# Index queries for the last 384 of 512 real tokens, in a one-core hybrid retention and sparse-attention block

## The chip, the cores and the metric

The kernel runs on one core of a Trainium2 chip. The metric is the device time of one execution in microseconds; the median of three runs is compared. Engines are named as in the profile: PE is the matrix engine (PEld its weight loads), DVE the vector engine, ACT the scalar engine, POOL the general engine, SP the queue that issues most loads.

## The reference

One layer on 512 real tokens behind 16 meta tokens (528 positions, width 1024), all in float32: a feed-forward block, a mixer, a second feed-forward block, a final norm. The mixer projects the normed input once with `w_in` and splits it into retention (rq, rk, rv, rg), attention (aq, ak, av), the index (iq, ik, iw) and two gates. What matters here is the index of the sparse attention:

```python
rel = jax.nn.relu(jnp.einsum('bqhd,bsd->bqhs', qib, ki))
score = jnp.einsum('bqh,bqhs->bqs', wib, rel).astype(jnp.float32) * idx_scale
admissible = (key_pos[None, :] >= N_META) & (key_pos[None, :] <= tq[:, None])
score = jnp.where(admissible[None], score, -jnp.inf)
_, sel = lax.top_k(score, k_top)          # k_top = min(256, 512 // 4) = 128
```

Each query keeps the 128 real keys with the highest scores among those at or before it, and always the meta keys. A query among the first 128 real tokens has at most 128 admissible keys, so it keeps them all, whatever their scores are. Index queries are 8 heads of 64, rotated by position (rope); the index key is one head of 64.

## The kernel before

Activations lie transposed, features on the partitions and tokens along the columns: `xs(k)` gives two tiles of 128 x 528 for each of 8 blocks of features, a high part `xh` and a remainder `xl`, so that a float32 product is made of three matmuls in a rounded format. Weights come as raw blocks of two column groups (`load_w`, issued on SP, two buffers `raw`) and are split by `split_w` into `whi` (ACT, line 117) and `wlo` (DVE, line 118), three buffers each. `mm3` (line 152) then runs, for one group of 128 output features, 8 x 3 matmuls into one PSUM tile. `REAL = slice(NM, T)` picks the columns of the 512 real tokens.

The kernel runs feed-forward 1, then the index projections, then retention over 4 heads, attention over 8 heads, the output projections and feed-forward 2. The order of PE's instructions is the order of the program text (a manual schedule for PE); those of the other engines are ordered by the framework's scheduler, with its own priorities, and then run in that order.

The index stage (lines 565 to 600) is this. PE projects four groups of index queries (`psiq`), each two heads, and keeps all four in the four banks of the pool `sm`. Between them stand the pieces of the mixer's norm: after the first group ten small matmuls `psn` (line 204) sum the squares `ssum` that POOL has added up; DVE and POOL make the reciprocal roots (lines 211, 213), DVE spreads them on a diagonal (218, 222) and it is split; after the third group four matmuls `psn` (line 228) turn it into `R`, which ACT copies out (line 229). POOL multiplies the rope tables `cos` and `sin` with `R` (527, 528). `rope_swap` then rotates each group: four copies of swapped halves on ACT (547, 548), a product with cos on DVE (549) that ends the use of the bank, a product with sin on POOL (550), a sum on DVE (551); `split` makes `iqh` and `iql` of it. Then follow the index keys and the head weights, projected together (`psik`), and rotated likewise into `ikh` and `ikl`.

`index_steps` computes the scores later, a step at a time between the projections of retention (`psrq`, `psrk`, `psrg`, `psrv`), only for the query blocks j = 3, 2, 1 of 128 tokens, and `select_steps` picks the top 128 by 16 rounds of eight maxima for the same three blocks. Block 0 needs neither: its bias is the causal mask. So the first 128 columns of each index query are computed and never read.

Of the kernel before, what the change touches and what calls it, by code (L numbers as in the profile page):

```python
# [12 lines left out]
F32R = mybir.dt.float32r  # L13
# [5 lines left out]
P = 128  # L19
D = 1024  # L20
KD = D // P
S = 512
NM = 16
T = S + NM
# [57 lines left out]
def kernel(ctx: ExitStack, tc: tile.TileContext, x, meta, g1, wg1, wu1, wd1, gm,  # L82
# [53 lines left out]
    def split_w(v, eng=nc.vector):  # L136
        nk, n = v.shape[1], v.shape[2]
        hi = wpool.tile([P, 1024 + WPAD], F32R, tag="whi", name="whi", bufs=3)[:, w_at[0] :]
        lo = wpool.tile([P, 1024 + WPAD], F32R, tag="wlo", name="wlo", bufs=3)[:, w_at[0] :]
        hv = hi[:, : nk * n].rearrange("p (k c) -> p k c", k=nk)  # L140
        lv = lo[:, : nk * n].rearrange("p (k c) -> p k c", k=nk)
        split(v, hv, lv, eng)
        return hv, lv

    def mm3(outs, w, xs, nk, first=True, last=True):

        wh, wl = w
        for k in range(nk):
            xh, xl = xs(k)
            for i, (a, b) in enumerate(((wh, xh), (wh, xl), (wl, xh))):  # L150
                for o, sl in outs:
                    nc.tensor.matmul(o, a[:, k, :], b[:, sl], start=first and k == 0 and i == 0,  # L152
                                     stop=last and k == nk - 1 and i == 2)
# [21 lines left out]
    def new_x(k, at=0):  # L175

        h = xpool.tile([P, TX], F32R, tag=f"xh{k}", name=f"xh{k}")[:, at : at + T]
        l = xpool.tile([P, TX], F32R, tag=f"xl{k}", name=f"xl{k}")[:, at : at + T]
        xs_now[k] = (h, l)
        return h, l  # L180

    def xs(k):
        return xs_now[k]

    REAL = slice(NM, T)

    def halves(t, cut=TH):

        a, b = t[:, 512 - cut : 512], t[:, 512 : 512 + T - cut]
        return [(a, slice(0, cut)), (b, slice(cut, T))], t[:, 512 - cut : 512 - cut + T]  # L190
# [45 lines left out]
    def add_square(h, ssum, first, tpool, n=T, bufs=2, eng=nc.gpsimd):  # L236
        if first:
            nc.scalar.activation(ssum[:, :n], h, AF.Square)
        else:
            sq = tpool.tile([P, wide(n)], F32, tag="sq", name="sq", bufs=bufs)  # L240
            nc.scalar.activation(sq[:, :n], h, AF.Square)
            eng.tensor_tensor(ssum[:, :n], ssum[:, :n], sq[:, :n], ALU.add)
# [13 lines left out]
    with pool("f1") as fp, pool("gps", 2, PSUM) as gps, ExitStack() as later:  # L256
# [5 lines left out]
        def mm_tile(name):  # L262

            i = mm_count[0]
            mm_count[0] += 1
            return mm_pools[i % len(mm_pools)].tile([P, 1024], F32, tag="mm", name=name)
# [106 lines left out]
        with tc.manual_schedule(engines={mybir.EngineType.PE, mybir.EngineType.Activation, mybir.EngineType.DVE}):  # L373
            pss = [mm_tile("psg"), mm_tile("psg")]
# [87 lines left out]
        for f0, nf in ((0, 12), (12, 10)):  # L462
            hid = []
            for f in range(f0, f0 + nf, 2):
                cg = slice(f * P, (f + 2) * P)
                if f:
                    raw = load_w(wg1[:, cg], KD, 2 * P)
                    pss = []
                    for i in range(2):
                        w = split_w(raw[:, :, i * P : (i + 1) * P])  # L470
                        ps = mm_tile("psg")
# [15 lines left out]
                for i in range(2):  # L487
                    if f:
                        w = split_w(raw[:, :, i * P : (i + 1) * P])
                        ps = mm_tile("psu")  # L490
                        mm3(halves(ps)[0], w, xs, KD)
                    else:
                        ps = psus[i]
# [7 lines left out]
            for c in range(0, KD, 2):  # L501
                pss = [mm_tile("psd") for _ in range(2)]
                for kk in range(2):
                    r0 = (f0 + kk * nk) * P
                    raw = load_w(wd1[r0 : r0 + nk * P, c * P : (c + 2) * P], nk, 2 * P)
                    for i in range(2):
                        w = split_w(raw[:, :, i * P : (i + 1) * P])
                        mm3(halves(pss[i])[0], w, lambda k: hid[kk * nk + k], nk, kk == 0, kk == 1)
                for i in range(2):
                    k = c + i  # L510
                    nc.vector.scalar_tensor_tensor(hT[k], halves(pss[i])[1], 0.5, hT[k], ALU.mult, ALU.add)
                    if f0:
                        h, l = new_x(k, XO)
                        split_gain(hT[k], gains[:, 1, k : k + 1], h, l)
                        add_square(hT[k], ssum2, k == 0, fp, bufs=4)
                        nc.scalar.dma_start(hd[k], hT[k][:, REAL])
    R = R2
    Rr = R[:, REAL]
    w_at[0] = 0
# [15 lines left out]
    def sm_tile(name):  # L535
        return smp.tile([P, S], F32, tag="sm", name=name)
# [4 lines left out]
    def rope_swap(ps, cos, sin, half, n):  # L541

        a, b = tmp(), tmp()
        av, bv = a[:, :n], b[:, :n]
        for r in range(0, P, 2 * half):
            lo, hi = slice(r, r + half), slice(r + half, r + 2 * half)
            nc.scalar.activation(bv[hi], ps[lo], AF.Copy)
            nc.scalar.activation(bv[lo], ps[hi], AF.Copy)
        nc.vector.tensor_tensor(av, ps, cos, ALU.mult)
        nc.gpsimd.tensor_tensor(b[:, :n], b[:, :n], sin, ALU.mult)  # L550
        nc.vector.tensor_tensor(a[:, :n], a[:, :n], b[:, :n], ALU.add)
        return a[:, :n]
# [9 lines left out]
    ix = ixs.enter_context(pool("ix", 1, side="right"))  # L562


    with pool("ixt") as ixt:
        tp.update(pool=ixt, bufs=8)
        norm = rstd_steps(ssum2, T, D, R2, ixt, lambda: mm_tile("psn"))
        pss = []
        cols = Cols(w_in, OFF_IQ, 4)
        for i in range(4):  # L570
            w = cols.next()
            ps = sm_tile("psiq")
            mm3([(ps, REAL)], w, xs, KD)
            pss.append(ps)
            if i < 3:
                next(norm)
        cos, sin = rope_tables(0, ixt)
        iq = []
        for i in range(4):
            y = rope_swap(pss[i], cos[:, REAL], sin[:, REAL], 32, S)  # L580
            h = ix.tile([P, S], F32R, tag=f"iqh{i}", name="iqh")
            l = ix.tile([P, S], F32R, tag=f"iql{i}", name="iql")
            split(y, h, l)
            iq.append((h, l))
        w = Cols(w_in, OFF_IK, 1).next()
        ps = sm_tile("psik")
        mm3([(ps, REAL)], w, xs, KD)
        a, y = tmp(), tmp()
        nc.scalar.activation(y[32:64, :S], ps[0:32], AF.Copy)
        nc.scalar.activation(y[0:32, :S], ps[32:64], AF.Copy)  # L590
        nc.vector.tensor_tensor(a[0:64, :S], ps[0:64], cos[0:64, REAL], ALU.mult)
        iw = ix.tile([IH, S], F32, tag="iw", name="iw")
        nc.vector.tensor_tensor(iw, ps[64:72], R[64:72, REAL], ALU.mult)
        nc.gpsimd.tensor_tensor(y[0:64, :S], y[0:64, :S], sin[0:64, REAL], ALU.mult)
        nc.vector.tensor_tensor(y[0:64, :S], a[0:64, :S], y[0:64, :S], ALU.add)
        ikh = ix.tile([P, S], F32R, tag="ikh", name="ikh")
        ikl = ix.tile([P, S], F32R, tag="ikl", name="ikl")
        for r in (0, 64):
            nc.scalar.activation(ikh[r : r + 64], y[0:64, :S], AF.Copy)
            nc.vector.tensor_tensor(ikl[r : r + 64], y[0:64, :S], ikh[0:64].bitcast(F32), ALU.subtract)  # L600
    wt = bp.tile([P, 4, IH], F32, tag="wt", name="wt")

    def index_steps():
        psw = sm_tile("psw")
        for j in range(1, 4):
            nc.tensor.transpose(psw[:, j * IH : (j + 1) * IH], iw[:, j * P : (j + 1) * P], ident[:IH, :IH])
        nc.scalar.activation(wt[:, 1:4, :], psw[:, IH : 4 * IH].rearrange("p (j h) -> p j h", h=IH),
                             AF.Copy, scale=float(np.float32(ID**-0.5) * np.float32(IH**-0.5)))
        for j in (3, 2, 1):
            n = P * (j + 1)  # L610
            for h0 in range(0, IH, 2):
                qh, ql = iq[h0 // 2]
                qs = slice(j * P, (j + 1) * P)
                pair = [sm_tile("pssc") for _ in range(2)]
                for i, (a, b) in enumerate(((qh, ikh), (qh, ikl), (ql, ikh))):
                    for ps, r in zip(pair, (0, 64)):
                        nc.tensor.matmul(ps[:, :n], a[r : r + 64, qs], b[r : r + 64, :n], start=i == 0, stop=i == 2)
                for h, ps in enumerate(pair, h0):
                    rel = tmp()
                    nc.scalar.activation(rel[:, :n], ps[:, :n], AF.Relu)  # L620
                    nc.vector.scalar_tensor_tensor(
                        score[j], rel[:, :n], wt[:, j, h : h + 1],
                        caus[:, S - n :] if h == 0 else score[j], ALU.mult, ALU.add)
                    yield
# [52 lines left out]
    with pool("rt") as rt:  # L677
        tp.update(pool=rt, bufs=7)
        cos, sin = rope_tables(2, rt)
# [201 lines left out]
    with pool("ao") as ao:  # L881
        ao_parts = []
        with pool("at") as at:
            tp.update(pool=at, bufs=8)
            cos, sin = rope_tables(1, at)
# [109 lines left out]
        with pool("ou") as ou:  # L995
# [5 lines left out]
            for c in range(KD):  # L1001
                w = cols.next()
                ps = sm_tile("psga")
# [6 lines left out]
            for c in range(KD):  # L1010
                w = cols.next()
                ps = sm_tile("psat")
# [11 lines left out]
    with pool("om") as ou:  # L1024
# [10 lines left out]
        for c in range(KD):  # L1035
            hc = ou.tile([P, S], F32, tag="hc", name="hc", bufs=4)
            nc.scalar.dma_start(hc, hd[c])
            w = cols.next()
            ps = sm_tile("psmo")
# [4 lines left out]
            h, l = new_x(c)  # L1044
# [10 lines left out]
        for i in range(2):  # L1055
            w = split_w(raw0[:, :, i * P : (i + 1) * P])
# [13 lines left out]
    with pool("f2") as fp, pool("f2ps", 8, PSUM) as f2ps:  # L1070
# [30 lines left out]
        for f0, nf in ((0, 12), (12, 10)):  # L1101
            hid = []
            for f in range(f0, f0 + nf, 2):
                cg = slice(f * P, (f + 2) * P)
                if f:
                    raw = load_w(wg2[:, cg], KD, 2 * P)
                    ps = [bank("psg") for _ in range(2)]
                else:
                    ps = ps0
                st = []  # L1110
                for i in range(2):
                    if f:
                        w = split_w(raw[:, :, i * P : (i + 1) * P])
# [7 lines left out]
                ps = [bank("psu") for _ in range(2)]  # L1121
                for i in range(2):
                    w = split_w(raw[:, :, i * P : (i + 1) * P])
# [7 lines left out]
            for c in range(2):  # L1131
                cs = slice(c * 512, (c + 1) * 512)
                pss = [bank("psd") for _ in range(4)]
# [48 lines left out]
```

## Time and profile before

| | |
|---|---|
| median of 3 runs | 1594.84 us (1594.56 to 1595.37) |
| the profiled execution | 1595.39 us |
| its span | 1593.5 us, granted PE clock 0.999 |
| PE, DVE, ACT, POOL busy | 99%, 52%, 36%, 15% of the span |
| index stage, psiq to psik's start | 397.4 to 421.1 us |
| moved by DMA | 148.66 MB, mean 93 GB/s |

A row of the timeline gives start, duration in us, engine, line, operation, `out<-in` by tile names, then the array's rows and columns in use, the moving operand's partitions x columns, and the count; in brackets the engine's idle time before and what ended it. Matmul durations are modelled and overlap each other; a matmul's cost is read from the distance between starts. A row of a group ends with total busy us, mean ns of one, and idle time before it.

### The profile page before, as it was taken

The numbers are of one execution on the slowest core, as the hardware profiler recorded it, in microseconds if no ns is written. First come the engines' busy times: TensorE is split into PE (matmuls) and PEld (weight loads), VectorE is DVE, ScalarE is ACT, GpSimd is POOL, SyncE is SP. The second block draws the span as 40 slices with busy tenths as digits, with TensorE's granted clock in tenths as the row PEclk, the third lists the DMA queues.
The fourth block names the chain that finished last, engine by engine and source line by source line (L and its number), as shares of the span: only waits on it lengthen the run. The fifth ranks groups of instructions, "written<-read, shape, count | busy, mean of one in ns | idle before, by whom it ended". The sixth has DMA issues, their size and how long they took to land.

```text
span 1593.5 us, 23010 instructions
## 1 busy us (share of the span) xinstructions
PE 1582.4 (99%) x9731; PEld 1421.5 (89%) x9731; DVE 820.9 (52%) x1263; ACT 570.6 (36%) x912; POOL 232.7 (15%) x187
## 2 busy tenths in 40 slices
PE   9999999999999999999999999999999999999998
PEld 8999999999888898899898999988888888888886
DVE  5443234334575776866845666753454434324434
ACT  6322222233544333233333555553234323223223
POOL 1211001111320200301304210011002111001100
PEclk9999999999999999999999999999999999999999
DMA  5222232224332132231312322313243322232222
GB/s 185 90 84 83 93 113 80 97 80 143 108 112 67 42 116 78 80 116 40 119 54 72 112 69 66 94 58 103 80 138 101 118 96 89 89 113 90 93 91 81
DMA packets 148582, 148.66 MB, mean 93 GB/s; under 512 B 3288, under 2 KB 137456, under 8 KB 148480
## 3 DMA queue, kind: packets, MB, share of 16 engines
q1 hardware_dynamic: 143872, 138.16, 26.9%
q10 hardware_dynamic: 4544, 9.03, 1.7%
q8 instruction: 76, 1.25, 0.3%
q14 instruction: 26, 0.21, 0.0%
q0 software_dynamic: 64, 0.01, 0.0%
HBM read 143.00 MB, written 4.19 MB: 92 GB/s over the span
## 4 chain that ended last, share of the span: by engine, by line
PE 91%; DVE 4%; ACT 2%; issue 1%; POOL 1%; DMA 1%; ACTq 0%; POOLq 0%; DVEq 0%
PE psu L152 15%; PE psg L152 15%; PE psd L152 8%; PE psd L1143 7%; PE psrv L152 6%; PE psrg L152 6%; PE psrk L152 3%; PE psgate L152 3%; PE psmo L152 3%; PE psat L152 3%; PE psga L152 3%; PE psak L152 3%; PE psav L152 3%; PE psrq L152 2%; PE psro L152 2%; PE psaq L152 2%
## 5 line engine op out<-in xcount | busy, mean ns | idle before, releaser
L117 ACT ACTIVATE whi<-raw 128x1024 fp32r<-128x1024 f32 (+3 forms) x284 | 277.7, 979 | 841.8 <-PE psu L152 165.6
L118 DVE TENSOR_TENSOR wlo<-raw,whi 128x1024 fp32r<-128x1024 f32 (+3 forms) x284 | 338.6, 1192 | 179.0 <-ACT whi L117 175.3
L152 PE MATMUL psu<-xl,whi 128*128 128x264 f32 (+1 forms) x528 | 141.0, 319 | 0.0
L152 PE MATMUL psu<-xh,whi 128*128 128x264 f32 (+1 forms) x528 | 140.6, 318 | 0.0
L152 PE MATMUL psu<-xh,wlo 128*128 128x264 f32 (+1 forms) x528 | 140.6, 318 | 0.0
L152 PE MATMUL psg<-xl,whi 128*128 128x264 f32 (+1 forms) x496 | 133.3, 321 | 0.0
L152 PE MATMUL psg<-xh,wlo 128*128 128x264 f32 (+1 forms) x496 | 132.8, 321 | 0.0
L152 PE MATMUL psg<-xh,whi 128*128 128x264 f32 (+1 forms) x496 | 132.8, 320 | 0.0
L152 PEld LDWEIGHTS psu<-xh,wlo 128*128 128x128 f32 x528 | 88.1, 188 | 6.9
L152 PEld LDWEIGHTS psu<-xh,whi 128*128 128x128 f32 x528 | 87.8, 188 | 6.8
L152 PEld LDWEIGHTS psu<-xl,whi 128*128 128x128 f32 x528 | 87.4, 188 | 6.9
L152 PEld LDWEIGHTS psg<-xh,wlo 128*128 128x128 f32 x496 | 82.6, 188 | 6.9
L152 PEld LDWEIGHTS psg<-xh,whi 128*128 128x128 f32 x496 | 82.3, 188 | 6.7
L152 PEld LDWEIGHTS psg<-xl,whi 128*128 128x128 f32 x496 | 82.0, 188 | 6.8
L483 POOL TENSOR_TENSOR t<-t,R 128x528 f32<-128x528 f32 x22 | 37.5, 1707 | 262.3 <-ACT t L482 262.3
L1118 POOL TENSOR_TENSOR t<-t,R 128x512 f32<-128x512 f32 x22 | 38.4, 1748 | 251.6 <-ACT t L1117 251.6
L152 PE MATMUL psd<-hl,whi 128*128 128x264 f32 x352 | 71.3, 284 | 0.0
L152 PE MATMUL psd<-hh,wlo 128*128 128x264 f32 x352 | 70.8, 283 | 0.0
L152 PE MATMUL psd<-hh,whi 128*128 128x264 f32 x352 | 70.6, 282 | 0.0
L1143 PE MATMUL psd<-whi,hh 128*128 128x512 f32 x176 | 68.5, 389 | 0.0
L1143 PE MATMUL psd<-wlo,hh 128*128 128x512 f32 x176 | 68.5, 389 | 0.0
L1143 PE MATMUL psd<-whi,hl 128*128 128x512 f32 x176 | 68.5, 389 | 0.0
(316 smaller groups left out, 3555.8 us busy)
## 6 DMA issues: line engine op xcount, KB each, us to landing
raw<-in_w_in_dram SPq DMA_DIRECT2D x34, 1024.0 KB, 4.9
raw<-in_ffn_w_up_dram SPq DMA_DIRECT2D x22, 1024.0 KB, 5.0
raw<-in_ffn_w_gate_dram SPq DMA_DIRECT2D x21, 1024.0 KB, 5.0
raw<-in_w_in_dram SPq DMA_DIRECT2D x25, 512.0 KB, 3.5
raw<-in_ffn_w_down_dram SPq DMA_DIRECT2D x10, 1024.0 KB, 4.8
raw<-in_w_ret_out_dram SPq DMA_DIRECT2D x16, 512.0 KB, 3.4
raw<-in_ffn_w_down_dram SPq DMA_DIRECT2D x8, 768.0 KB, 4.3
raw<-in_ffn_w_down_dram SPq DMA_DIRECT2D x8, 640.0 KB, 3.9
```

Of the source, the lines that this page charges most:

```text
L117: nc.scalar.activation(hi, src, AF.Copy)
L118: eng.tensor_tensor(lo, src, hi.bitcast(F32), ALU.subtract)
L152: nc.tensor.matmul(o, a[:, k, :], b[:, sl], start=first and k == 0 and i == 0, stop=last and k == nk - 1 and i == 2)
L483: nc.gpsimd.tensor_tensor(t, t, R, ALU.mult)
L1118: nc.gpsimd.tensor_tensor(t, t, R, ALU.mult)
L1143: nc.tensor.matmul(pss[b], a[:, bs], m[:, k % 2, :], start=k0 + k == 0 and i == 0, stop=k0 + k == nf - 1 and i == 2)
```

## The change

The index queries are projected, rotated and split for the last 384 real tokens alone. The moving operand of the 96 `psiq` matmuls starts 128 columns later and is 384 columns wide instead of 512; so are the copies, products, sums and casts of the four groups, and the tiles `iqh` and `iql`. The scores read the same queries under a slice shifted by 128. Index keys, head weights, scores and selection are as before.

```diff
     REAL = slice(NM, T)
+
+    LATE = slice(NM + P, T)
+    NL = S - P
...
-            ps = sm_tile("psiq")
-            mm3([(ps, REAL)], w, xs, KD)
+            ps = sm_tile("psiq")[:, :NL]
+            mm3([(ps, LATE)], w, xs, KD)
...
-            y = rope_swap(pss[i], cos[:, REAL], sin[:, REAL], 32, S)
-            h = ix.tile([P, S], F32R, tag=f"iqh{i}", name="iqh")
-            l = ix.tile([P, S], F32R, tag=f"iql{i}", name="iql")
+            y = rope_swap(pss[i], cos[:, LATE], sin[:, LATE], 32, NL)
+            h = ix.tile([P, NL], F32R, tag=f"iqh{i}", name="iqh")
+            l = ix.tile([P, NL], F32R, tag=f"iql{i}", name="iql")
...
-                qs = slice(j * P, (j + 1) * P)
+                qs = slice((j - 1) * P, j * P)
```

## The prediction

> **What bounds the kernel now.** I read the page first: busy time by engine, then the chain that ended last.
>
> ```profile
> PE 1582.4 (99%) x9731; PEld 1421.5 (89%) x9731; DVE 820.9 (52%) x1263; ACT 570.6 (36%) x912; POOL 232.7 (15%) x187
> ...
> PE 91%; DVE 4%; ACT 2%; issue 1%; POOL 1%; DMA 1%; ACTq 0%; POOLq 0%; DVEq 0%
> ```
>
> TensorE (PE) is busy for 99% of the span, and 91% of the chain is its matmuls; there is one weight load for each matmul. What PE no longer has to stream comes off the end, unless something that fed it in time now comes too late. So the stage of the change has to be read closely. The timeline of PE from 397 us on:
>
> ```profile
> 397.42 0.40 PE L152 MATMUL psiq<-xh,whi 128*128 128x512 f32 x1
> ...
> 402.65 0.40 PE L152 MATMUL psiq<-xh,wlo 128*128 128x512 f32 x1
> 402.88 1.17 PE L204 MATMUL psn<-ones,ssum 128*128 128x1 f32 x10
> ...
> 414.92 0.75 PE L228 MATMUL psn<-tmp,ones_r 128*128 128x512 f32 x4
> ...
> 421.09 0.39 PE L152 MATMUL psik<-xh,whi 128*128 128x512 f32 x1
> ...
> 432.20 0.39 PE L152 MATMUL psrq<-xl,whi 128*128 128x512 f32 x1
> 432.74 0.50 PE L152 MATMUL psrq<-xh,wlo 128*128 128x512 f32 x1
> ```
>
> First column: start; second: modelled duration, which overlaps the next one, so what a matmul costs is the distance between starts. The first index-query group takes 402.88 - 397.42 = 5.46 us for 24 matmuls, 0.2275 each. PE goes through four groups, the two small psn pieces of the norm, psik and psrq without a gap, up to one: the matmul due at 432.20 + 0.23 = 432.43 starts at 432.74, 0.31 late. The list of waits names what it waited for:
>
> ```profile
> PEld psrq L152 <- DVE wlo L118: 0.6, 1, 0.6
> ```
>
> **The term that is removed.** 96 matmuls (4 tiles x 8 k x 3 parts) go from 512 to 384 columns. No matmul of that shape with 128 rows stands in this trace; the same timeline has 400 and 272 columns in one stretch:
>
> ```profile
> 464.49 0.34 PE L751 MATMUL psst<-rqh,rkh 128*128 128x400 f32 x1
> ...
> 465.57 0.29 PE L751 MATMUL psst<-rqh,rkh 128*128 128x272 f32 x1
> ...
> 466.31 0.28 PE L751 MATMUL psst<-rqh,rkh 128*128 128x256 f32 x1
> ```
>
> Six of 400 columns take 465.57 - 464.49 = 1.08 us, 0.180 each; six of 272 take 0.74, 0.123 each. That is 0.44 ns a column between 272 and 400, and (0.2275 - 0.180) / 112 = 0.42 between 400 and 512: one straight line. At 384 it gives 0.180 - 16 x 0.43 ns = 0.173. The saving is 96 x (0.2275 - 0.173) = 5.2 us. The ends: not less than if 384 cost what 400 costs, 96 x 0.0475 = 4.6; not more than 96 x 128 x 0.44 ns = 5.4. I take 5.2, since 384 is nearest to the row of 400 and three rows agree on the slope. The distance of 0.123 also says that a weight load, though it lasts longer, does not set the pace:
>
> ```profile
> L152 PEld LDWEIGHTS psu<-xh,wlo 128*128 128x128 f32 x528 | 88.1, 188 | 6.9
> ```
>
> [...]
>
> **What PE now reaches earlier, in order.** Each time below is the old one minus what PE has saved by then.
>
> *The column sums.* The rows of the weight load that PE does ahead of psn, and of the POOL add that makes its operand:
>
> ```profile
> 402.65 1.32 PEld L204 LDWEIGHTS psn<-ones,ssum 128*128 128x128 f32 x10
> ```
> ```profile
> 399.79 1.82 POOL L242 TENSOR_TENSOR ssum<-ssum,sq 128x528 f32<-128x528 f32 x1 [1.82 <-ACT sq L241]
> ```
>
> The first group now ends 24 x 0.0545 = 1.3 us earlier; the weight load is due at 401.34, but ssum is complete at 401.61. A wait that was covered by streaming is uncovered: 0.27 plus a signal, so 0.3 us, with every later matmul queued behind it. Bounds: 0 (if the load need not come so early: the matmul itself is due at 401.57) to 0.6. From here all of PE is 1.0 earlier, after psiq 1 and 2 (0.055 x 48 = 2.6 more) 3.6, and after psiq 3, at psik, 5.2 - 0.3 = 4.9.
>
> *The norm and the first bank.* psik needs the bank of psiq 0 (four banks, all held by psiq), which is free once its product with cos is done; cos needs R:
>
> ```profile
> 402.85 1.06 ACT L117 ACTIVATE whi<-raw 128x1024 fp32r<-128x1024 f32 x1 [3.20 <-PE psiq L152]
> ...
> 406.43 0.65 ACT L117 ACTIVATE tmp<-tmp 128x528 fp32r<-128x528 f32 x1 [2.52 <-DVE tmp L222]
> ...
> 414.88 1.06 ACT L117 ACTIVATE whi<-raw 128x1024 fp32r<-128x1024 f32 x1 [4.30 <-PE psiq L152]
> 415.96 0.61 ACT L229 ACTIVATE R<-psn 128x528 f32<-128x528 f32 x1
> ...
> 422.89 0.63 ACT L117 ACTIVATE iqh<-tmp 128x512 fp32r<-128x512 f32 x1 [3.89 <-DVE tmp L551]
> 423.55 0.59 ACT L547 ACTIVATE tmp<-psiq 32x512 f32<-32x512 f32 x1
> ...
> 429.58 1.04 ACT L117 ACTIVATE whi<-raw 128x1024 fp32r<-128x1024 f32 x1
> ```
> ```profile
> 416.65 1.73 POOL L527 TENSOR_TENSOR cos<-cos,R 128x528 f32<-128x528 f32 x1 [11.13 <-DMA raw<-in_w_in_dram]
> ...
> 429.10 1.30 POOL L550 TENSOR_TENSOR tmp<-tmp,sin 128x512 f32<-128x512 f32 x1 [1.79 <-ACT tmp L548]
> ```
> ```profile
> 406.30 1.22 DVE L118 TENSOR_TENSOR wlo<-raw,whi 128x1024 fp32r<-128x1024 f32 x1
> ...
> 418.42 0.69 DVE L549 TENSOR_TENSOR tmp<-psiq,cos 128x512 f32<-128x512 f32 x1 [1.22 <-POOL cos L527]
> ...
> 430.87 0.68 DVE L551 TENSOR_TENSOR tmp<-tmp 128x512 f32<-128x512 f32 x1
> 431.47 1.21 DVE L118 TENSOR_TENSOR wlo<-raw,whi 128x1024 fp32r<-128x1024 f32 x1
> ...
> 442.75 0.69 DVE L688 TENSOR_TENSOR tmp<-psrq,sin 128x512 f32<-128x512 f32 x1 [0.59 <-POOL sin L528]
> ```
>
> The split of 414.88 waits for PE's end of psiq 2, R stands behind it on ACT and needs psn of 414.92: both move by 3.6, so R moves to 412.35. The bank was free at 418.42 + 0.69 = 419.11, 2.0 before psik at 421.09; now it is free at 415.4 against a need at 416.2. The cover shrinks to 0.8 and holds. Two loads could eat it. The split needs the raw block of rq, whose load starts when the split of 406.30 ends (407.52) and took about 4.2; that split follows the column sums, so it moves by only 1.0, the block lands near 410.7, and it is wanted at 411.3. And by the two builds' instruction lists, which are equal in number and order on PE, DVE, POOL and SP, ACT takes its issue of the cos load after the split that it stood ahead of (that of 402.85, which waits for PE, now about 401.7) and its issue of the sin load after the norm's own split (that of 406.43, now 405.4): they go out near 402.8 and 406.
>
> ```profile
> DMA to landing us min/median/max: 3.5/4.2/4.8
> ```
> ```profile
> cos<-in_rope_dram ACTq DMA_DIRECT2D x2, 264.0 KB, 2.7
> sin<-in_rope_dram ACTq DMA_DIRECT2D x2, 264.0 KB, 2.9
> ```
>
> They land near 405.5 and 409, while POOL wants cos at 413.0: nothing lost. The sin load shares the engines with the block of rq, so that may come up to 1 us late (a quarter of the block's bytes): R then moves by 3.1 instead of 3.6 and the bank still holds. Nothing of it reaches PE directly.
>
> *The second half of rq's weights.* This is the one wait that PE has here. The weights end at 431.47 + 1.21 = 432.68; PE will ask at 432.43 - 4.9 = 427.5. Their chain starts at R (3.6 earlier) and passes work that shrinks with the columns: on ACT two iqh casts and eight copies between 422.89 and 429.05, each 0.63 - 0.11 (0.63 at 512 and 1.06 at 1024 make 0.84 ns an element), 1.1 in all; on DVE two or three steps of 0.69, less 0.13 each by 1.22 at 1024, 0.3; on POOL two products of 1.30, less nothing or a quarter, 0 to 0.6. So the weights move by 3.6 + 1.4 to 2.0 = 5.0 to 5.6 against PE's 4.9: the wait of 0.31 falls to 0.2 or goes, a gain of 0.1 to 0.3. I take 0.2. If R is 0.5 late as above, the wait becomes up to 0.7 and 0.4 is lost.
>
> *After that.* The first index scores need the bank of psrq 0, free after the product of 442.75 (443.44) and used at about 444.0. That product hangs on the same chain, which has by then moved by 5.0 or more; so has PE. The scores read the same 128 columns of each query under a shifted slice, with the same number and size of matmuls; the selection and all that follows start from PE as before. Off the bound, ACT loses 20 x 0.11 and DVE 12 x 0.13 us: worth nothing in time.
>
> The sum: -5.2 + 0.3 - 0.2 = -5.1 us. The profiled execution took 1595.39 (span 1593.5 and 1.9 around it) and would take 1590.3; it lies 0.55 above the median of the three runs, 1594.84, so that becomes **1589.7**. Its own range: at best 5.4 + 0.3 = 5.7, so 1589.1; at worst 4.6 - 0.6 = 4.0, so 1590.8; with 0.4 for how the runs scatter, 1588.7 to 1591.2.
>
> **Rivals.** *B, the weight load sets a floor.* If 384 columns could not be spaced closer than a weight load's 188 ns, the saving is 96 x 0.0395 = 3.8, the wait at the column sums mostly goes, and the result is near 1591.0. For it: the load's 188 lies above 173, and loads are busy for 89%. Against: 272 columns at 123. [...]
>
> *C, the chain through R does not follow PE.* The profile itself puts POOL's cos at 416.65 down to the landing of a raw weight block, not to R. Were that so, cos would stay, the first bank would be free at 419.0, and PE would stand at psik from 416.2, 2.8 us; then rq's weights come at about 431.0 for a need at 430.3, 0.4 more of a wait than before. Left over is 4.9 - 2.8 - 0.4 = 1.7: 1593.1. Against it: cos reads no weights, and R ended at 416.57, 0.08 before. A late block of rq would be a weaker form. Chance 0.08.
>
> *D, slower: the wait of C also costs PE its pace.* The timeline's start shows what a matmul costs after PE has stood:
>
> ```profile
> 1.46 4.63 PE L318 MATMUL psg<-idle 128*128 128x512 f32 x10 [1.46 <-DVE idle L286]
> ...
> 7.25 1.64 PE L318 MATMUL psg<-idle 128*128 128x512 f32 x6
> ```
>
> Ten take 4.63, 0.46 each, twice 0.2275; six somewhat later take 1.64. If the 24 matmuls of psik ran at 0.46 after 2.8 us of standing, they would cost 24 x 0.23 = 5.5 more, and the total is -1.7 + 5.5 = +3.8: 1598.6. It outweighs the saving from 8 such matmuls on. It needs C first, and every shorter wait in this stage is followed by the full pace (0.31 at 432.74). [...] Chance 0.04.
>
> That the change does not do what it says can be left out: the built program has 96 matmuls of 128x384.
>
> **How the numbers follow.** A measurement of this kernel tells about 0.2%, 3.2 us, from no change. The forecast has 0.84, all of it faster; B 0.02 faster and 0.02 same; C 0.08 same; D 0.04 slower. That makes 0.86, 0.10 and 0.04. The range takes the forecast's own, 0.1 more below for a steeper slope, and above three fifths of C's loss, for a chain that follows PE only in part: 1588.6 to 1591.8.
>
> **What would show it.** Psiq starts 0.173 apart; psn at 401.9; R at 412.4 (if it stays near 416, C); psik at 416.2 without a gap; at most 0.2 before the third matmul of the second psrq; the first index score 5.0 earlier, and every later stage by the same amount to the end. Wrong would be a spacing at or above 0.188 (B), a gap before psik (C), matmuls of 0.46 (D), or a later stage that takes the lead back.

## The result: 1591.13 us, and the profile after

The changed kernel takes 1591.13 us (median of 9 runs, 1589.76 to 1592.10) against 1595.37 (9 runs, 1594.56 to 1595.52): a ratio of 0.9973, 95% interval 0.9963 to 0.9983, 4.2 us faster. Forecast were 5.1 us and 1589.7. The profiled execution took 1590.52 (span 1588.7). From its page, the busy line and the chain by engine:

```profile
PE 1576.4 (99%) x9731; PEld 1419.7 (89%) x9731; DVE 820.0 (52%) x1263; ACT 569.3 (36%) x912; POOL 230.9 (15%) x187
...
PE 94%; DVE 3%; ACT 1%; issue 1%; POOL 1%; DMA 0%; ACTq 0%; POOLq 0%; DVEq 0%
```

PE is as full as before. The timeline of PE, the same places as were shown of before:

```profile
396.50 0.34 PE L152 MATMUL psiq<-xh,whi 128*128 128x384 f32 x1
...
400.52 0.34 PE L152 MATMUL psiq<-xh,wlo 128*128 128x384 f32 x1
400.75 1.28 PE L207 MATMUL psn<-ones,ssum 128*128 128x1 f32 x10
...
410.31 0.75 PE L231 MATMUL psn<-tmp,ones_r 128*128 128x512 f32 x4
...
414.98 0.34 PE L152 MATMUL psiq<-xh,wlo 128*128 128x384 f32 x1
...
416.54 0.47 PE L152 MATMUL psik<-xh,whi 128*128 128x512 f32 x1 [1.22 <-DVE tmp L552]
...
428.42 0.40 PE L152 MATMUL psrq<-xl,whi 128*128 128x512 f32 x1
428.66 0.39 PE L152 MATMUL psrq<-xh,wlo 128*128 128x512 f32 x1
...
432.98 0.40 PE L152 MATMUL psrk<-xh,whi 128*128 128x264 f32 x2
...
439.12 0.50 PE L620 MATMUL pssc<-ikh,iqh 64*128 64x512 f32 x2
```

The two last places in the kernel before:

```profile
437.85 0.40 PE L152 MATMUL psrk<-xh,whi 128*128 128x264 f32 x2
...
443.99 0.50 PE L617 MATMUL pssc<-ikh,iqh 64*128 64x512 f32 x2
```

This execution reached the stage 0.92 us earlier (396.50 against 397.42) though nothing ahead of it is changed. The lead is there in the first microseconds of the program: the six warm-up matmuls that the prediction shows at 7.25 start here at 6.36:

```profile
6.36 1.64 PE L321 MATMUL psg<-idle 128*128 128x512 f32 x6
```

The other profiles reach the stage between 396.64 and 397.24, all ahead of the one of the kernel before. As the program does not differ there, I take this for scatter and count from the first index-query matmul, written with a plus. The spacing is (400.52 - 396.50) / 23 = 0.175. The last psiq matmul would have been followed by psik at 414.98 + 0.17 = 415.15, but psik starts at 416.54, after 1.22 us of idle time. The wait in the second psrq is gone (0.24 between 428.42 and 428.66). The first index score is at +42.62 instead of +46.57; from there to the end it is 1149.6 us in the one and 1149.5 in the other. So by this pair of profiles the change is made in this stage, 3.95 us, and what follows keeps it. In the second profile of the changed kernel, below, the stretch from the first index score to the end takes 1150.5 us, 1.0 more, so single executions also differ outside the stage. The list of waits of PE's loads and of PE has two new entries:

```profile
PEld psik L152 <- ACT tmp L551: 1.5, 1, 1.5
...
PEld psn L207 <- POOL ssum L245: 0.2, 1, 0.2
```

The first is the new gap (the list names ACT's copies; the row of psik names the product on DVE, which ends later), the second the uncovered column sums. What stands behind the gap, on ACT:

```profile
404.41 0.34 ACTq L529 DMA_DIRECT2D sin<-in_rope_dram  x1
...
412.30 1.06 ACT L117 ACTIVATE whi<-raw 128x1024 fp32r<-128x1024 f32 x1 [4.17 <-DMA raw<-in_w_in_dram]
413.39 0.61 ACT L232 ACTIVATE R<-psn 128x528 f32<-128x528 f32 x1
```

and on DVE:

```profile
404.27 1.22 DVE L118 TENSOR_TENSOR wlo<-raw,whi 128x1024 fp32r<-128x1024 f32 x1
...
415.84 0.56 DVE L552 TENSOR_TENSOR tmp<-psiq,cos 128x384 f32<-128x384 f32 x1 [1.21 <-POOL cos L530]
...
426.56 1.22 DVE L118 TENSOR_TENSOR wlo<-raw,whi 128x1024 fp32r<-128x1024 f32 x1
```

Before, the split of rq waited for PE; now it waits for its block. The block's buffer came free at 404.27 + 1.22 = 405.49, and the split starts at 412.30, 6.8 us later. In the kernel before, the sin load went out 4.7 us ahead of that request (402.85 against 407.52), now 1.1 us (404.41 against 405.49):

```profile
402.85 0.34 ACTq L526 DMA_DIRECT2D sin<-in_rope_dram  x1
```

R starts as that split ends, the product with cos frees the first bank at 415.84 + 0.56 = 416.40, and psik follows 0.14 later.

### The profile page after: what moved, and what is told of

Read it like the earlier page. It is cut to its first block, busy times and chain, and to the rows that moved or that the text cites. A ratio compares the mean times of both kernels' runs of the same rounds, so it can differ in the third digit from the quotient of the medians.

```text
span 1588.7 us, 23011 instructions
## 1 busy us (share of the span) xinstructions
PE 1576.4 (99%) x9731; PEld 1419.7 (89%) x9731; DVE 820.0 (52%) x1263; ACT 569.3 (36%) x912; POOL 230.9 (15%) x187
## 3 DMA queue, kind: packets, MB, share of 16 engines
q8 instruction: 76, 1.25, 0.3%
## 4 chain that ended last, share of the span: by engine, by line
PE 94%; DVE 3%; ACT 1%; issue 1%; POOL 1%; DMA 0%; ACTq 0%; POOLq 0%; DVEq 0%
PE psu L152 16%; PE psg L152 15%; PE psd L152 8%; PE psd L1146 7%; PE psrv L152 6%; PE psrg L152 6%; PE psrk L152 3%; PE psak L152 3%; PE psav L152 3%; PE psrq L152 3%; PE psgate L152 3%; PE psro L152 3%; PE psmo L152 3%; PE psaq L152 3%; PE psat L152 3%; PE psga L152 3%
```

## The experiments

The kernels ran in two groups, each on one chip beside the kernel before: sin load earlier, psik in another pool, R on DVE and sin loaded twice beside 1595.86 us, the other four beside 1596.03. The theory: the sin load, which now goes out when rq's block is requested, makes that block late; R is behind its split; PE meets it at the first bank. Times in the table are from each profile, from the first index-query matmul; "split" is rq's, "weights" the end of the second psrq's wlo, "gap" the distance before psik less a normal 0.17 (0.23 at 512 columns). The times alone do not tell the changed versions apart where they differ by about 1 us: the 95% interval of a ratio to the kernel before is 1.4 to 2.1 us wide to either side. What tells them apart is where PE stands in the traces, one profile of each version and two of the changed kernel.

| kernel | median us | less than before, same group | split | R | psik (gap) | weights | psrk |
|---|---|---|---|---|---|---|---|
| before | 1595.86 and 1596.03 | | 17.46 | 18.55 | 23.68 (0) | 35.27 | 40.44 |
| changed, again | 1591.50 | 4.5 | 15.59 | 16.68 | 19.83 (1.2) | 31.05 | 36.27 |
| sin load earlier | 1590.38 | 5.5 | 14.31 | 15.39 | 18.65 (0) | 29.77 | 35.04 |
| psik in another pool | 1591.03 | 4.8 | 15.53 | 16.61 | 18.64 (0) | 31.00 | 36.17 |
| R on DVE | 1590.57 | 5.3 | 15.34 | 14.58 | 18.64 (0) | 29.66 | 35.01 |
| sin loaded twice | 1592.91 | 3.0 | 16.26 | 17.35 | 20.47 (1.8) | 31.67 | 36.97 |
| rest narrow, matmuls wide | 1595.13 | 0.9 | 17.46 | 18.55 | 23.68 (0) | 30.41 | 40.00 |
| matmuls narrow, rest wide | 1593.90 | 2.1 | 15.88 | 16.97 | 20.26 (1.2) | 33.65 | 38.83 |
| sin earlier and R on DVE | 1589.90 | 6.1 | 14.13 | 14.58 | 18.65 (0) | 29.61 | 35.01 |

**The sin load one place earlier.** Here the text of the changed kernel issues both loads where the stage opens (`table_loads` holds the two `dma_start`); in this stage the scheduler then leaves every other instruction in its place.

```diff
...
+        tables = table_loads(0, ixt)
         norm = rstd_steps(ssum2, T, D, R2, ixt, lambda: mm_tile("psn"))
...
-        cos, sin = rope_tables(0, ixt)
+        cos, sin = rope_tables(0, ixt, tables)
```

> Edit: the changed kernel, with ACT's issue of the sin load one place earlier, right behind the cos load and ahead of the norm's own split; nothing else moves on any engine. Times are counted from the first index-query matmul (in the changed kernel: split of rq +15.8, R +16.9, psik +20.0 with 1.2 to 1.4 us of standing before it). Theory: the block of rq comes late because the sin load runs beside it; R stands behind that block's split on ACT, and the first bank behind R. Then the block lands about 4.9 us after its request, at +13.9, R comes at +15.0, the bank is free at +18.0, psik starts at +18.7 with no gap, the wait before the second psrq's third matmul stays away, and the kernel gains 1.4 us on the changed one: about 1589.7. Rival (the block is late by its own request, which hangs on the column sums, and the sin load does not matter): the gap stays over 1 us and the time at 1591.1.

PE's and ACT's timeline of this kernel:

```profile
396.86 0.34 PE L152 MATMUL psiq<-xh,whi 128*128 128x384 f32 x1
...
415.51 0.39 PE L152 MATMUL psik<-xh,whi 128*128 128x512 f32 x1
```
```profile
401.61 0.46 ACTq L529 DMA_DIRECT2D sin<-in_rope_dram  x1
...
411.17 1.06 ACT L117 ACTIVATE whi<-raw 128x1024 fp32r<-128x1024 f32 x1 [2.69 <-DMA raw<-in_w_in_dram]
412.25 0.61 ACT L232 ACTIVATE R<-psn 128x528 f32<-128x528 f32 x1
```

The split is at +14.31, 0.4 later than expected (5.3 us from the buffer's release, not 4.9), but the cover holds: psik at +18.65 without a gap, as the theory has it, and psrk is reached at +35.04 instead of +36.27. By the medians 5.5 us are gained instead of 4.5, a difference within the intervals. Moving one DMA issue past one instruction takes the gap away, so the late sin load caused it.

**psik in a bank of another pool.**

```diff
-        ps = sm_tile("psik")
+        ps = mm_tile("psik")[:, :S]
```

> Edit: the changed kernel, with psik in a tile of the other PSUM pool, which is free, so that it needs no bank of psiq. Instructions and their order are the same on every engine. Rival (the bank alone is what costs): psik at +18.7, no gap, 1.4 us gained, about 1589.7. Theory (the late R is what costs, and the bank is only where PE meets it first): psik at +18.7 without a gap, but the weights of the second psrq, which hang on the same R, still end at about +31.3, while PE now asks for them at +30.0: the wait moves there, 1.2 us, and the time stays near 1591.0.

```profile
415.59 0.39 PE L152 MATMUL psik<-xh,whi 128*128 128x512 f32 x1
...
426.75 0.40 PE L152 MATMUL psrq<-xl,whi 128*128 128x512 f32 x1
428.00 0.50 PE L152 MATMUL psrq<-xh,wlo 128*128 128x512 f32 x1 [0.85 <-DVE wlo L118]
```

The gap before psik is gone and stands in the second psrq instead: 428.00 - 426.75 = 1.25, of which 0.23 is normal. psrk is reached at +36.17 against +36.27. So the bank was only the place where PE meets the delay; that R carries it is shown by the next run.

**R copied out by DVE.**

```diff
-        nc.scalar.activation(dst, ps[:, :n], AF.Copy)
+        if dst is R2:
+            nc.vector.tensor_copy(dst, ps[:, :n])
+        else:
+            nc.scalar.activation(dst, ps[:, :n], AF.Copy)
```

> Edit: the changed kernel, with R copied out of PSUM by DVE instead of ACT, so that it no longer stands behind the split of rq. The block of rq lands as late as before. Theory: R starts when psn ends, near +14.8, is done at +15.5, the bank is free at +18.0, psik starts at +18.7 without a gap, the weights of the second psrq are ready at about +29.5 for a need at +30.0; 1.4 us gained, about 1589.7, with the split of rq still near +15.8. Rival (a late block holds PE in another way than through R): the gap stays, 1591.1.

ACT, DVE and PE of this kernel:

```profile
411.99 1.06 ACT L117 ACTIVATE whi<-raw 128x1024 fp32r<-128x1024 f32 x1 [3.71 <-DMA raw<-in_w_in_dram]
```
```profile
411.23 0.71 DVE L233 COPY R<-psn 128x528 f32<-128x528 f32 x1 [1.69 <-PE psn L231]
```
```profile
415.29 0.39 PE L152 MATMUL psik<-xh,whi 128*128 128x512 f32 x1
```

The block is as late as ever (its split at +15.34), yet R starts at +14.58 and PE has no gap. So here the block holds PE only through R's place in ACT's order.

**The sin table loaded twice.**

```diff
         nc.scalar.dma_start(s, rope[i, 1])
+        if i == 0:
+            s2 = mp.tile([P, T], F32, tag="sin2", name="sin2", bufs=1)
+            nc.scalar.dma_start(s2, rope[i, 1])
```

> Edit: the changed kernel, with the sin table loaded a second time, right behind the first, into a tile that nobody reads: the suspected cost doubled. Theory: the block of rq lands another 1.3 to 1.9 us later, R at +18.2 to +18.8, the gap before psik grows to 2.6 to 3.3 us, and the time goes to about 1592.6. Rival (the sin load does not matter): gap 1.2 to 1.4 us and 1591.1 as in the changed kernel.

```profile
413.03 1.06 ACT L117 ACTIVATE whi<-raw 128x1024 fp32r<-128x1024 f32 x1 [4.33 <-DMA raw<-in_w_in_dram]
```
```profile
417.24 0.47 PE L152 MATMUL psik<-xh,whi 128*128 128x512 f32 x1 [1.67 <-DVE tmp L555]
```

The direction is the theory's and the size is not: in the profile the split is 0.5 to 0.7 later than in the two profiles of the changed kernel, not 1.3 to 1.9, and the idle time is 1.67 us, not 2.6. By the medians the second load costs 1.6 us (2.95 gained instead of 4.53, again within the intervals); the profiled execution took 1592.20, 0.7 less than the median, so a part of the difference may lie in how the landing scatters.

**The changed kernel again.**

> The changed kernel itself, to stand beside the others on one chip. Expected of the theory: 4.2 us under the kernel before, with a gap before psik that follows the landing of rq's block from run to run (1.0 to 2.0 us); of a rival in which the gap is fixed by the order of instructions: 1.5 us in every profile.

```profile
416.79 0.47 PE L152 MATMUL psik<-xh,whi 128*128 128x512 f32 x1 [1.01 <-DVE tmp L552]
```

4.5 us less than the kernel before on this chip (ratio 0.9970, 0.9960 to 0.9981). The idle time is 1.01 us here and 1.22 in the first profile; two values do not settle whether it scatters. The times speak for it: with rq's block on PE's path they lie 2.3 to 3.5 us apart (changed kernel 2.3 and 2.8, psik in another pool 2.3, matmuls narrow with the rest wide 3.1, sin twice 3.5), without it 0.7 to 1.9 (both cures 0.7, R on DVE 1.2, sin earlier 1.4, rest narrow with wide matmuls 1.6, before 0.9 to 1.9). The numbers of runs differ (5 to 11, and up to 23 of before). That points to the landing; it does not prove it.

**The narrow work of the other engines alone.**

```diff
-            ps = sm_tile("psiq")[:, :NL]
-            mm3([(ps, LATE)], w, xs, KD)
-            pss.append(ps)
+            ps = sm_tile("psiq")
+            mm3([(ps, REAL)], w, xs, KD)
+            pss.append(ps[:, P:])
```

> Edit: one part of the change alone: the index-query matmuls stay 512 columns wide, while copies, products, sums, casts and tiles take the last 384. Theory: PE has nothing less to do; only the wait before the second psrq's third matmul (0.31 us) goes: 0.3 us under the kernel before, at most 0.4. Rival (part of the gain lies in the lighter ACT, DVE and POOL work by itself): over 1 us under.

psrk stands at +40.00 instead of +40.44: on PE the 0.31 wait and the slower restart behind it are gone, and nothing else. In time it can't be told from the kernel before (ratio 0.9995, 0.9986 to 1.0004). Why the wait is gone is not shown cleanly, because the scheduler also takes the split of these weights earlier, ahead of work of the third and fourth group that it followed in the kernel before:

```profile
424.68 1.04 ACT L117 ACTIVATE whi<-raw 128x1024 fp32r<-128x1024 f32 x1
```

That is +27.75, against +32.16 (429.58) before, so the weights' end at +30.41 instead of +35.27 is not the doing of the narrow work alone.

**The narrow matmuls alone.**

```diff
-            ps = sm_tile("psiq")[:, :NL]
-            mm3([(ps, LATE)], w, xs, KD)
+            ps = sm_tile("psiq")
+            nc.tensor.matmul(ps[:, :P], w[0][:, 0, :], xs(0)[0][:, NM : NM + P], start=True, stop=True)
+            mm3([(ps[:, P:], LATE)], w, xs, KD)
...
-            y = rope_swap(pss[i], cos[:, LATE], sin[:, LATE], 32, NL)
...
+            y = rope_swap(pss[i], cos[:, REAL], sin[:, REAL], 32, S)
...
-            iq.append((h, l))
+            iq.append((h[:, P:], l[:, P:]))
```

> Edit: the other part alone: the 96 matmuls are 384 wide (and four of 128 columns, 0.3 us, fill the first columns of each bank so that they are defined), while copies, products, sums, casts and tiles stay 512 wide. The prediction's side remark (the lighter work of the other engines lies off the bound and is worth nothing): 4.2 - 0.3 = 3.9 us under the kernel before. Theory (once PE is 3.6 us ahead, the chain from R to the weights of the second psrq is what PE waits for, so its length counts): R at +17.1, weights 16.7 us later as in the kernel before, +33.8, for a need at +31.7: a wait of about 2 us, and only 1.5 us under the kernel before.

PE and DVE of this kernel:

```profile
417.50 0.47 PE L152 MATMUL psik<-xh,whi 128*128 128x512 f32 x1 [1.07 <-DVE tmp L552]
...
428.89 0.50 PE L152 MATMUL psrq<-xh,whi 128*128 128x512 f32 x1 [0.24 <-ACT whi L117]
429.22 0.40 PE L152 MATMUL psrq<-xl,whi 128*128 128x512 f32 x1
430.95 0.51 PE L152 MATMUL psrq<-xh,wlo 128*128 128x512 f32 x1 [1.32 <-DVE wlo L118]
```
```profile
429.68 1.21 DVE L118 TENSOR_TENSOR wlo<-raw,whi 128x1024 fp32r<-128x1024 f32 x1
```

Three gaps now: the one before psik, and two in the second psrq, which starts 0.4 us late for its `whi` (0.63 after the matmul ahead of it, at 428.26, not 0.23) and stands another 1.5 us (430.95 - 429.22 - 0.23) for its `wlo`. Together that is the wait of about 2 us that the theory expected; psrk is reached 1.6 us earlier than in the kernel before. The weights end at +33.65, 16.7 us after R, as in the kernel before; in the changed kernel it is 14.4. 2.1 us are gained instead of 4.5. The scheduler also orders a few ACT and DVE instructions after this place otherwise, so the 2.1 is not the gaps' doing alone; the gaps are in the trace. The remark in the prediction that the lighter ACT and DVE work is worth nothing in time fell, though the prediction's own paragraph on the weights had counted on that shorter chain: beside the narrow matmuls it is worth about 2 us (4.5 - 2.1, less the 0.4 by which the four added matmuls move the end of psiq), without them 0.4 by the trace and, by the median, 0.9 that can't be told from nothing.

**Both cures together.**

> Edit: the changed kernel with the sin load issued one place earlier and R copied out by DVE, both cures together. Theory: either cure alone already takes away the only wait, so both give the same as either: psik at +18.7, psrk at +35.0, 5.4 us under the kernel before, within 0.3 of each one alone. Rival (each cures a part of its own): 6 us or more under.

psrk is at +35.01, as with either cure (+35.04, +35.01), so they cure the same thing. The median is 6.1 us under before (ratio 0.9962, 0.9950 to 0.9975), more than the 5.4 of the theory and by that count the rival's; the trace of the stage has no third gain. The other 0.6 is not shown to be a gain at all: it lies inside the interval, and outside the stage single profiles differ by up to 0.9 us ahead of it and up to 1.0 behind it. At 1589.90 us it has the lowest median of the versions that were run; its interval overlaps that of the changed kernel (0.9960 to 0.9981).

## Why the prediction was right in direction and 0.9 us too high

The gain was forecast 0.9 us too high, and the time, 1589.7 against 1591.13, 1.4 us too low: the other 0.5 is the baseline, of which three runs had the median 1594.84 and nine have 1595.37.

- *The term that is removed.* Right. Spacing 0.175 for 0.173 forecast; with the first column sums' wait (0.2 by the list of waits, 0.3 forecast) the last psiq matmul moved from +23.45 to +18.48, 4.97 earlier, for 4.9 forecast. The weight-load floor (B) is refuted. In this stretch the busy share of weight loads rose to 1.00 (from 4.54 of 5.50 us, 0.83, in the first group before), and the spacing, 0.175, is still shorter than one load of 0.188: in this stretch a full row of loads is no floor. The half of B's chance that was put on "same" was the author's estimate: no run shows a spacing that would save less than the 3.2 us that can be told from no change; 0.175 saves 96 x (0.2275 - 0.175) = 5.0 us.

```profile
396.50:397.50 1.00, 1.00 (x8) 1.00 (x7) 0.71 (x1) 0.99 (x2) 0.54 (x1) 1.00 1.02 298
```

(Columns of this stretch: length, busy of PE, PEld, DVE, ACT, POOL with counts, granted clock, DMA share, GB/s.)

- *The norm and the first bank.* This step failed, by the size of one term, the landing of rq's block. It named the place, the split of rq, R behind it and the sin load beside the block, and then wrote that "the bank still holds". Both parts of the term were too small. For the block it took 4.2 us, the middle of the only two landings that its row of three loads has, 3.5 of half a block and 4.8 of a whole one; rq's own is not among them. The page of the kernel before had a nearer figure, the median of 34 whole blocks:

```profile
raw<-in_w_in_dram SPq DMA_DIRECT2D x34, 1024.0 KB, 4.9
```

For the collision it took at most 1 us. With 4.9 and the same 1 us the block would, by the prediction's own sum, land near 412.4, 1.1 after the split's due time of 411.3, against a cover of 0.8: the bank would not have held. Measured from the buffer's release to the split, a block alone takes 5.1 to 5.3 us (sin earlier, both cures) and one beside the sin load 6.4 to 6.9 (five profiles), so the collision costs 1.1 to 1.8. R moved by 1.7 us, not 3.6 or 3.1, and the cover of 0.8 became a gap. That is a half of rival C, which got 0.08: the chain through R followed PE only in part, by a late block, the form that C called weaker. C's own reading, that POOL's cos waits for a raw block, stays wrong: with R on DVE, cos starts at +15.4, 0.1 after R, 1.8 before the next block's first closing packet (+17.2).

- *The second half of rq's weights.* Right in the outcome (the wait of 0.31 is gone), for a partly wrong reason: the weights came 4.0 earlier, not 5.0 to 5.6, but PE was held at psik by 1.3 and asked later. With the gap cured, the weights come at +29.6 to +29.8 for a need at +30.0, as forecast.

- *After that.* Right by the first pair of profiles: from the first index score to the end nothing moved (1149.6 against 1149.5). The other profiles are 0.3 to 1.0 longer there, the second one of the changed kernel by the full 1.0, so this scatters with the kernel unchanged.

- *The sum.* -4.97 + 1.33 - 0.31 = -3.95 in the profiles against -5.1. The term left out is the 1.33 before psik; with it cured, 5.4 is reached in the stage (psrk from +40.44 to +35.04). That the gain of 4.2 lies within the forecast's own bounds, 4.0 to 5.7, is in part luck: the lower one was made of a smaller saving and a longer wait at the column sums, and neither came. Only the widening for C had a late chain in it.

D's condition, 2.8 us of standing, did not come about. After 1.0 to 1.7 us of standing the first matmul is followed 0.31 us later by the next, and those at 0.23, the full pace.

## What to carry to other kernels

When PE is full and a stage on it gets shorter, list every load that is requested in that stage from something that does not get shorter, and compare its landing with its new need; take the duration from loads of the same size, beside what will then run next to them (here 5.1 to 5.3 us for a block alone and 6.4 to 6.9 beside the sin load). A DMA issue that the scheduler moved by one instruction cost about a quarter of the saving here (1.3 of 5.0 us), and ACT, taking its work in order, passed the late load on to R, which does not need it: R started at +16.89, behind the split of +15.80, and on DVE at +14.58. So place such a copy on an engine that does not wait, or the load before the rush. Work off the critical path is worth nothing only as long as the path stays where it is: here the lighter ACT and DVE work was worth about 2 us beside the narrow matmuls, and 0.4 in the trace without them.

## What the runs showed of the hardware

Here a small load just ahead of a larger one delayed it. From the buffer's release to its split, rq's block of 1024 KB took 5.1 to 5.3 us alone and 6.4 to 6.9 beside the 264 KB sin load: 1.1 to 1.8 more, where the sin load's share by bytes, about a quarter of 5.1 to 5.3, would be an estimated 1.3. Alone, a 1024 KB block's sixteen closing packets ended within 0.45 to 0.61 us of each other (before, sin earlier, both cures, rest narrow with wide matmuls); with the 264 KB sin load issued 1.1 us ahead of its request they ended 1.4 to 2.2 us apart, 2.3 with two such loads, in the first profile of the changed kernel from +13.2 to +15.4, most by +14.1. The split started at +15.80, after the last of them. In that profile the sin load's packets ran from +8.9 to +10.4 and the block's from +10.1, so in the trace the two overlap by 0.3 us only. That is less than the 1.1 to 1.8 us of delay; why a few of the closing packets lag by that much is not settled by these runs.
